# A fourth buffer for incoming weights, paused state chunks, sooner means in the pooling, and seven products in one more MLP group

## The chip, the cores and the metric

The kernel runs on one core of a Trainium2 chip. The metric is the time on the device in microseconds (us), the median of several runs. The engines are called PE (TensorE, the matrix multiplier), PEld (its weight loads), DVE (VectorE), ACT (ScalarE), POOL (GpSimd) and SP (SyncE, which here only issues DMAs).

## The reference, cut to what matters

Two layers run over 520 columns: 512 tokens of a new prompt and one new token for each of 8 samples. D is 1024, FF is 4096, everything is fp32. Layer 0 mixes the tokens by a gated linear recurrence, layer 1 by causal means over 2, 4, 8 and 16 tokens; after either comes an MLP with a squared ReLU.

```python
def _mlp(x, norm_g, w_up, w_down):
    h = _rmsnorm(x, norm_g)
    a = jnp.square(jax.nn.relu(jnp.einsum('bld,df->blf', h, w_up)))
    return jnp.einsum('blf,fd->bld', a, w_down)

for layer in range(DEPTH):
    if layer % N_MIXERS == 0:
        y, s = _hgrn2(x, s_hgrn[j], ...)      # new recurrent state: 8 samples x 8 heads x 128 x 128
    else:
        y, h = _pool(x, hist_pool[j], ...)    # rmsnorm, means over 2, 4, 8, 16 tokens, per-group map
    x = x + y
    x = x + _mlp(x, mlp_norm[layer], mlp_up[layer], mlp_down[layer])
return _rmsnorm(x, final_norm), ...
```

The outputs are the normed x, the new recurrent states (prompt and samples) and the last normed rows of the pooling.

## The kernel before

**Products.** x lies in SBUF as 8 tiles of 128 rows by 520 columns. A weight chunk is a fp32 tile `w` of 128x1024 (512 KB), loaded from `wall`. To keep fp32 accuracy, ACT casts it to a high part `wh` (L221) and DVE subtracts that to get a low part `wl` (L216); the inputs `u` and `a` are split in the same way. One product of a chunk takes three matmuls (`mm3`, L347 to L351) for each of 8 row blocks and each of two halves of 260 columns: 48 matmuls of 128x260, into an accumulator `acc`, of which two exist (the pool `pa`).

**The MLP.** `mlp` (L889) takes FF in 4 groups of 8 tiles. A group has 8 up products into `t` and `a` (L907 to L910), and then 8 down products; each of these ends with `x <- x + acc` (L917), by which DVE empties an accumulator. Groups that the table `FAST` names make their up products by a seven-product scheme (`fast_part`, L919): two chunks, a pair, give seven weight combinations `wp` (`pair_parts`, L229 to L262, with DVE steps ws L245, ws L249, w L254, ws L257 and the split in `put`, ACT L238 and DVE L239), and the inputs give four sums `T` for each row block (`sums`, L849, spread over the group before). A pair of up products is then 7 `quarter` products of 12 matmuls instead of 2 of 48. `FAST` is (2, 3) for the first layer and (1, 2, 3) for the second: five of eight groups. The first up products of the second layer's MLP run column half by half beside the pooling's windows.

**What sets the order.** The PE order is the written order. So is SP's in most of the first layer's MLP (while `steady` is open): SP issues its DMAs one after the other, and one that must wait for a buffer or for data holds up all that stand behind it. DVE and ACT go in the order that a scheduler gives the written code; on the chip each is again a fixed queue. The written order comes from ticks: after every 12 matmuls (every quarter, or a quarter of a product) `tick` (L298) calls `top_up` (L268), which issues loads, splits or the next step of a weight pair, and advances the side tasks of `mix` (L105), each of which may ask to be called again some ticks later. Raw weights have three buffers (`rp`, L143); `top_up` loads a chunk when fewer than two raw chunks wait and fewer than three of the buffers are held (L280). Once a pair's two chunks are there, its steps are written.

**State chunks.** `new_states` (L695) is a side task beside the first layer's MLP. It updates the samples' states in 16 chunks. A chunk is: the load of `st` (L702) and two broadcast fills `bc` (L705) on SP; after STATE[0] ticks three POOL operations (L707 to L709); after STATE[1] more ticks the store `ss_o` (L711) on SP, with which the next chunk's loads are written at once. STATE is (7, 4).

**Pooling.** After the first layer's last down products, column half by half, `after_mlp0` (L1145) starts `pool_half(h)` three ticks after a half is done: the mean's matmul (L413), square root (L417) and reciprocal (L418), and then the windows (`windows`, L1078, from L1084 on), which DVE works through.

Of the kernel before, what the change touches and what calls it, by code (L numbers as in the profile page):

```python
# [7 lines left out]
F32 = mybir.dt.float32  # L8
# [22 lines left out]
SUMS = 2  # L31
SLOTS = 24
EXTRA = 2
FAST = (2, 3), (1, 2, 3)
PAIR = 2
# [3 lines left out]
SAMPLE, LAST_SAMPLE = (4, 4, 4, 1, 1), (5, 2, 3, 0, 1)  # L39
STATE = (7, 4)  # L40
EARLY = 2
# [97 lines left out]
def _kernel(ctx, tc, wall, xT, vec, kst, msk, s0, hist, y_o, sp_o, ss_o, pp_o, ps_o):  # L139
# [49 lines left out]
    depth = [DEPTH]  # L189

    def load():
        if order:
            i, parts = order.pop(0)
            if parts is None:
                w = pp.tile([P, NT, P], F32, name="poolw", bufs=2)
                pool_w.append(w)
            else:
                w = rp.tile([P, NT, P], F32, name="w")
                raw.append((w, parts))
            nc.sync.dma_start(w, wall[i].rearrange("p (k m) -> p k m", m=P))  # L200
# [67 lines left out]
    def top_up():  # L268
        while True:
# [6 lines left out]
            elif raw and raw[0][1] == PAIR and len(raw) > 1:  # L276
                making.append(pair_parts())
            elif raw and raw[0][1] != PAIR and ready() < depth[0] and (room >= 2 or not raw[0][1]):
                split()
            elif order and len(raw) < 2 and len(raw) + halved[0] + len(whole_w) + held_w[0] < 3:  # L280
                load()
            else:
                break
# [408 lines left out]

    drs = []

    def new_states():  # L695

        NH = NB // 2
        for h in range(H):
            for a in range(2):
# [4 lines left out]
                for n, t in ((1, tf), (2, tk)):  # L704
                    nc.sync.dma_start(t, drs[h][n * NB + a * NH:n * NB + (a + 1) * NH, :P].unsqueeze(0).broadcast_to([P, NH, P]))  # L705
                yield STATE[0]
                nc.gpsimd.tensor_tensor(st, st, tf, op=ALU.mult)  # L707
                nc.gpsimd.tensor_tensor(tk, tk, v8[:, h, b].unsqueeze(2).broadcast_to([P, NH, P]), op=ALU.mult)
# [134 lines left out]
    sctx, steady = ExitStack(), ExitStack()  # L843
    sn = sctx.enter_context(tc.tile_pool(name="states", bufs=1))
    states = [True]
    mix.spawn(new_states(), 8)
    steady.enter_context(tc.manual_schedule(engines={mybir.EngineType.SP}))

    def sums(ts, u, step):  # L849
# [6 lines left out]

        def whole_part(k, h, name):
            f = pair_pool[0].tile([P, HT], F32, name=name)
            nc.vector.tensor_tensor(f, *(p[:, span(h)] for p in u[k]), op=ALU.add)  # L859
            return f  # L860

        for j in range(NT // 2):
            b12, f = whole_part(j, 1, "b12"), whole_part(j, 0, "b11")
            nc.vector.tensor_tensor(f, b12, f, op=ALU.subtract)
            put(0, f)
            yield step
            b22 = whole_part(j + NT // 2, 1, "b22")
            nc.vector.tensor_tensor(f, b22, f, op=ALU.subtract)
# [4 lines left out]
            yield step  # L873
            b21 = whole_part(j + NT // 2, 0, "b22")
            nc.vector.tensor_tensor(b21, b21, f, op=ALU.subtract)
# [13 lines left out]
    def mlp(u, r, after, full, fast, apart=None, between=None):  # L889

        ts = [[] for _ in range(4)]
        for g in range(NF // G):
            if g == fast[0] - 1 and not apart:
                open_pairs()
# [66 lines left out]
            if g in fast:  # L961
                assert len(ts[3]) == NT // 2
                for m in range(0, G, 2):
                    fast_part(m)
            elif g == 0 and apart:
                for h in range(2):
# [10 lines left out]
            else:  # L977
                for m in range(G):
                    up_part(m, None)()
            last = g == NF // G - 1  # L980
            if last:
# [3 lines left out]
            if g == 0 and apart:  # L985
                close_pool()
                open_pairs()
                mix.spawn(sums(ts, u, 1), 2)
            for m in range(full if last else NT):
# [155 lines left out]
    def after_mlp0(m, h):  # L1145
# [5 lines left out]
        if len(done[h]) == NT:  # L1151
            mix.spawn(pool_half(h), 3)

# [99 lines left out]
```

## Time and profile before

| | before |
| --- | --- |
| time, median of 3 runs | 1107.88 us (1107.70 to 1108.51) |
| profiled execution: its own time | 1108.78 us |
| profiled execution: span, mean granted clock | 1107.0 us, 0.988 |
| PE matmuls busy | 1063.3 us (96%) |
| PE weight loads busy | 1041.9 us (94%) |
| DVE busy | 790.8 us (71%) |
| ACT busy | 509.9 us (46%) |
| POOL busy | 96.9 us (9%) |
| DMA traffic | 128.11 MB, mean 116 GB/s |

The profile is of one execution; its times are counted from the start of the span. A row of the timeline gives start, duration, engine, line, operation, `out<-in` and shape; in brackets stands how long the engine had been idle before it and which event ended that. "SPq" is the issue of DMAs from SP's queue. In the windows "x" counts instructions and PEclk is the mean granted clock of PE, 1.00 being 2.4 GHz. In the first layer's MLP group 0 has its up products up to about 381 and its down products up to about 427; group 1 goes on to 526, group 2 to 622, group 3 to about 721.

### The profile page before, as it was taken

How to read it: one execution, taken by the hardware profiler on the slowest of the kernel's cores; microseconds unless marked ns; L12 is line 12 of the kernel's file. 1: busy time of each engine (PE TensorE's matmuls, PEld its weight loads, DVE VectorE, ACT ScalarE, POOL GpSimd, SP SyncE). 2: the span in 40 equal slices, each digit the busy share in tenths (PEclk: the TensorE clock that was granted, in tenths of full speed). 3: DMA queues.
4: the chain of work that ended last, by engine and by line, in shares of the span. 5: the costliest groups of instructions: out<-in, count | busy, mean ns of one | idle time of the engine just before them, and what ended most of it. 6: DMA issues, size and time to landing. Idle time of an engine off the chain costs nothing. (4 is left out here: it accounts for less than half of the span.)

```text
span 1107.0 us, 21169 instructions
## 1 busy us (share of the span) xinstructions
PE 1063.3 (96%) x8458; PEld 1041.9 (94%) x8458; DVE 790.8 (71%) x1652; ACT 509.9 (46%) x1174; POOL 96.9 (9%) x145
## 2 busy tenths in 40 slices
PE   9899999899999999999998999997999999999996
PEld 8899999889999999999998999986999999999996
DVE  7898888888679543547864785789958747847845
ACT  6545554444455422332551465546626625625642
POOL 1011101010001221223121000000000000000000
PEclk9999999999999999998999999998999999999998
DMA  8233233223234573464363245034422422422312
GB/s 272 78 99 118 81 98 111 78 87 113 74 104 120 165 228 93 138 203 131 115 210 107 75 131 174 20 99 152 152 77 97 138 73 95 120 85 70 130 38 78
DMA packets 67170, 128.11 MB, mean 116 GB/s; under 512 B 8256, under 2 KB 36608, under 8 KB 67072
## 3 DMA queue, kind: packets, MB, share of 16 engines
q1 hardware_dynamic: 67072, 126.77, 36.0%
q8 instruction: 66, 1.08, 0.4%
q14 instruction: 32, 0.26, 0.1%
HBM read 119.71 MB, written 7.50 MB: 115 GB/s over the span
## 5 line engine op out<-in xcount | busy, mean ns | idle before, releaser
L351 PE MATMUL acc<-u,wh 128*128 128x260 f32 x1344 | 222.9, 288 | 1.1 <-ACT u L389 0.8
L351 PE MATMUL acc<-a,wh 128*128 128x260 f32 x1120 | 183.4, 286 | 7.8 <-DVE x L917 4.2
L351 PEld LDWEIGHTS acc<-u,wh 128*128 128x128 f32 x1344 | 185.2, 188 | 2.5 <-ACT u L389 1.0
L216 DVE TENSOR_TENSOR wl<-w,wh 128x512 fp32r<-128x512 f32 x216 | 149.1, 722 | 30.9 <-ACT wh L221 30.5
L351 PEld LDWEIGHTS acc<-a,wh 128*128 128x128 f32 x1120 | 156.7, 192 | 8.4 <-DVE x L917 4.4
L221 ACT CAST wh<-w 128x512 fp32r<-128x512 f32 x216 | 122.5, 617 | 66.5 <-DMA w<-wall 47.4
L351 PE MATMUL acc<-u,wl 128*128 128x260 f32 x672 | 134.9, 282 | 0.0
L351 PE MATMUL acc<-a,wl 128*128 128x260 f32 x560 | 114.1, 286 | 0.0
L351 PEld LDWEIGHTS acc<-u,wl 128*128 128x128 f32 x672 | 103.2, 188 | 0.0
L351 PEld LDWEIGHTS acc<-a,wl 128*128 128x128 f32 x560 | 87.9, 192 | 0.0
L351 PE MATMUL acc<-T,wp 128*128 128x260 f32 x600 | 81.0, 284 | 2.8 <-ACT R L932 2.8
L917 DVE TENSOR_TENSOR x<-x,acc 128x520 f32<-128x520 f32 x48 | 33.3, 693 | 68.6 <-PE acc L351 68.4
L351 PEld LDWEIGHTS acc<-T,wp 128*128 128x128 f32 x600 | 75.3, 188 | 3.8 <-ACT R L932 3.2
L351 PE MATMUL acc<-a,wx 128*128 128x260 f32 x624 | 76.8, 282 | 0.0
L351 PEld LDWEIGHTS acc<-a,wx 128*128 128x128 f32 x624 | 75.6, 188 | 0.0
L351 PE MATMUL pr<-a,wh 128*128 128x260 f32 x384 | 72.6, 290 | 1.1 <-ACT a L942 0.7
L351 PEld LDWEIGHTS pr<-a,wh 128*128 128x128 f32 x384 | 60.8, 192 | 1.9 <-ACT a L942 0.9
L238 ACT CAST wp<-w 128x512 fp32r<-128x512 f32 x60 | 36.1, 618 | 44.1 <-PE acc L351 43.2
L351 PE MATMUL pr<-a,wl 128*128 128x260 f32 x192 | 54.8, 285 | 0.0
L941 ACT ACTIVATE t<-t 128x260 f32<-128x260 f32 x80 | 32.5, 418 | 46.6 <-DVE t L940 46.4
L568 DVE COPY_PREDICATED A<-mt,pr 128x192 f32<-128x192 uint8 x144 | 47.4, 356 | 7.2 <-PE pr L563 3.9
L238 ACT CAST wp<-ws 128x512 fp32r<-128x512 f32 x50 | 30.4, 619 | 43.9 <-PE acc L351 22.3
(244 smaller groups left out, 2002.7 us busy)
## 6 DMA issues: line engine op xcount, KB each, us to landing
w<-wall SPq DMA_DIRECT2D x179, 512.0 KB, 3.4
st<-s SPq DMA_DIRECT2D x32, 256.0 KB, 3.7
bc<-rows SPq DMA_DIRECT2D x32, 256.0 KB, 6.8
bc<-rows SPq DMA_DIRECT2D x16, 258.0 KB, 3.5
ss_o<-st SPq DMA_DIRECT2D x16, 256.0 KB, 4.2
x<-xT SPq DMA_DIRECT2D x8, 260.0 KB, 5.3
y_o<-y SPq DMA_DIRECT2D x8, 260.0 KB, 2.7
poolw<-wall SPq DMA_DIRECT2D x2, 512.0 KB, 4.4
```

What stands on the lines that cost most here:

```text
L216: nc.vector.tensor_tensor(wl[:, k], w[:, k], wh[:, k], op=ALU.subtract)
L221: nc.scalar.copy(wh[:, k], w[:, k])
L238: nc.scalar.copy(w[:, k[0]], t)
L351: nc.tensor.matmul(o, lhs[a], r[b], start=first and n == 0, stop=last and n == 2, skip_group_check=more)
L568: nc.vector.copy_predicated(Av[:, jj * kk:(jj + 1) * kk, d:4, :].rearrange("p k s b -> p k (s b)"), mv[:, :, s:s + n, :].rearrange("p k s ...
L917: nc.vector.tensor_tensor(xs, xs, acc, op=ALU.add)
L941: nc.scalar.activation(t, t, AF.Square)
```

## The change

- The raw weights get a fourth buffer, `wr` (RAWS), from the pool of the state chunks, in turn with the three of `w`; `top_up` counts four buffers, so one chunk more may wait. At the first layer's last group it is taken back.
- `FAST` of the first layer becomes (1, 2, 3): group 1 also goes by seven products, six of eight groups in all. Its pairs, and the sums of the inputs, are therefore made during group 0.
- While a group's seven products are written, the list `busy` is not empty, and `new_states` asks again every tick before it writes a chunk's POOL operations.
- STATE goes from (7, 4) to (4, 3): a chunk takes 7 ticks instead of 11.
- The pooling's means start 2 ticks (first half) and 1 tick (second half) after a half is done, instead of 3.
- The second layer's sums of the inputs start 7 ticks after the first group's up products instead of 2, and take their scratch from the tile `R` of the pool `mp`.

```diff
+RAWS = 1
-FAST = (2, 3), (1, 2, 3)
+FAST = (1, 2, 3), (1, 2, 3)
-STATE = (7, 4)
+STATE = (4, 3)
...
+    raws = [lambda: rp.tile([P, NT, P], F32, name="w")] * 3
+    loads = [0]
...
-                w = rp.tile([P, NT, P], F32, name="w")
+                w = raws[loads[0] % len(raws)]()
+                loads[0] += 1
...
-            elif order and len(raw) < 2 and len(raw) + halved[0] + len(whole_w) + held_w[0] < 3:
+            elif order and (order[0][1] is not None or pp) and len(raw) < len(raws) - 1 and len(raw) + halved[0] + len(whole_w) + held_w[0] < len(raws):
...
+    busy = []
...
                 yield STATE[0]
+                while busy:
+                    yield 1
                 nc.gpsimd.tensor_tensor(st, st, tf, op=ALU.mult)
...
     sn = sctx.enter_context(tc.tile_pool(name="states", bufs=1))
+    raws += [lambda: sn.tile([P, NT, P], F32, name="wr", bufs=RAWS)] * RAWS
+    loads[0] %= 3
...
-        def whole_part(k, h, name):
-            f = pair_pool[0].tile([P, HT], F32, name=name)
+        def whole_part(k, h):
+            f = mp.tile([P, HT], F32, name="R", bufs=3)
...
         for g in range(NF // G):
+            last = g == NF // G - 1
+            if last and len(raws) > 3:
+                del raws[3:]
+                loads[0] %= 3
...
+                busy.append(True)
                 for m in range(0, G, 2):
                     fast_part(m)
+                busy.clear()
...
-                mix.spawn(sums(ts, u, 1), 2)
+                mix.spawn(sums(ts, u, 1), 7)
...
-            mix.spawn(pool_half(h), 3)
+            mix.spawn(pool_half(h), 2 - h)
```

**SP's queue, first layer, group 0's down products.** Here `w<-wall` and `wr<-wall` are weight loads, `st<-s` and `bc<-rows` the fills of a state chunk, `ss_o<-st` its store. Of the kernel before, from the fourth store on:

```order
L200 DMA w<-wall 128x1024 x2
L711 DMA ss_o<-st 128x512
L702 DMA st<-s 128x512
L705 DMA bc<-rows_1370 128x4x128 x2
L200 DMA w<-wall 128x1024 x3
L711 DMA ss_o<-st 128x512
L702 DMA st<-s 128x512
L705 DMA bc<-rows_1370 128x4x128 x2
L200 DMA w<-wall 128x1024 x3
L711 DMA ss_o<-st 128x512
```

Of the changed kernel, the first store here is the fifth; the loads of one `w` and one `wr` behind it and its fills are the first pair of group 1's, and the two loads in the last row, behind the seventh store, are its second:

```order
L719 DMA ss_o<-st 128x512
L708 DMA st<-s 128x512
L711 DMA bc<-rows_1370 128x4x128 x2
L205 DMA w<-wall 128x1024
L205 DMA wr<-wall 128x1024
L719 DMA ss_o<-st 128x512
L708 DMA st<-s 128x512
L711 DMA bc<-rows_1807 128x4x128 x2
L719 DMA ss_o<-st 128x512
L708 DMA st<-s 128x512
L711 DMA bc<-rows_1807 128x4x128 x2
L205 DMA w<-wall 128x1024 x2
```

Before, two or three weight loads stand between one state store and the next; now there are two or none, and the loads of a pair of group 1 stand behind a store and its fills.

**DVE's queue, the same place.** `x<-x,acc` empties the accumulator of a down product, `wl` is the low part of a weight, `ws`, `w<-w` and `wr<-w` are steps of a weight pair and `wp` its low parts. Of the kernel before, from the first emptying on:

```order
L216 TENSOR_TENSOR wl<-w,wh 128x512 x4
L917 TENSOR_TENSOR x<-x,acc 128x520
L216 TENSOR_TENSOR wx<-w,wx 128x512 x2
L216 TENSOR_TENSOR wl<-w,wh 128x512 x2
L917 TENSOR_TENSOR x<-x,acc 128x520
L216 TENSOR_TENSOR wl<-w,wh 128x512 x2
L917 TENSOR_TENSOR x<-x,acc 128x520
L216 TENSOR_TENSOR wl<-w,wh 128x512 x2
L917 TENSOR_TENSOR x<-x,acc 128x520
```

Of the changed kernel, from the second emptying to the fourth:

```order
L931 TENSOR_TENSOR x<-x,acc 128x520
L244 TENSOR_TENSOR wp<-w,wp 128x512
L250 TENSOR_TENSOR ws<-wr 128x512
L254 TENSOR_TENSOR ws<-ws,w 128x512
L259 TENSOR_TENSOR wr<-w,wr 128x512
L931 TENSOR_TENSOR x<-x,acc 128x520
L244 TENSOR_TENSOR wp<-ws,wp 128x512 x2
L262 TENSOR_TENSOR ws<-w,ws 128x512
L931 TENSOR_TENSOR x<-x,acc 128x520
```

And from the fifth to the sixth:

```order
L931 TENSOR_TENSOR x<-x,acc 128x520
L221 TENSOR_TENSOR wl<-w,wh 128x512 x2
L244 TENSOR_TENSOR wp<-w,wp 128x512
L250 TENSOR_TENSOR ws<-w 128x512
L259 TENSOR_TENSOR w<-w 128x512
L931 TENSOR_TENSOR x<-x,acc 128x520
```

Steps of weight pairs, each of which reads raw chunks that SP loads, now stand between the emptyings: `ws<-wr` (L250) of the first pair ahead of the third emptying, and `ws<-w` (L250) of the second pair ahead of the sixth.

**PE's queue, at the pooling.** `pr<-u,w` are the second layer's first products in fp32 matmuls (L363 of before), `pr<-sqs,mean_w` the means and `acc<-zp,poolw` the pooling's maps. Of the kernel before, from the first layer's last product on:

```order
L351 MATMUL pr<-a,wx 128x260 x24
L363 MATMUL pr<-u_8157,w 128x260 x8
L413 MATMUL pr<-sqs,mean_w 128x260
L1069 MATMUL acc<-zp,poolw 128x268 x4
L363 MATMUL pr<-u_8157,w 128x260 x4
L413 MATMUL pr<-sqs,mean_w 128x260
L363 MATMUL pr<-u_8157,w 128x260 x4
L1069 MATMUL acc<-zp,poolw 128x268 x4
L363 MATMUL pr<-u_8157,w 128x260 x48
```

Of the changed kernel, from the same product on:

```order
L356 MATMUL pr<-a,wx 128x260 x24
L368 MATMUL pr<-u_8241,w 128x260 x4
L418 MATMUL pr<-sqs,mean_w 128x260 x2
L368 MATMUL pr<-u_8241,w 128x260 x4
L1084 MATMUL acc<-zp,poolw 128x268 x4
L368 MATMUL pr<-u_8241,w 128x260 x8
L1084 MATMUL acc<-zp,poolw 128x268 x4
L368 MATMUL pr<-u_8241,w 128x260 x48
```

The two matmuls of the means now stand side by side, where eight matmuls of the next product and four of a map lay between them.

## Rows read from the trace of the kernel before

**Rows 1.** The page: span, busy time by engine, and the weight loads.

```profile
span 1107.0 us, 21169 instructions
PE 1063.3 (96%) x8458; PEld 1041.9 (94%) x8458; DVE 790.8 (71%) x1652; ACT 509.9 (46%) x1174; POOL 96.9 (9%) x145
...
w<-wall SPq DMA_DIRECT2D x179, 512.0 KB, 3.4
```

**Rows 2.** Timeline of PE, where its three longest waits in this MLP end.

```profile
500.13 1.20 PE L351 MATMUL acc<-a,wh 128*128 128x260 f32 x4 [3.61 <-ACT wp L238]
...
555.36 1.71 PE L351 MATMUL acc<-T,wp 128*128 128x260 f32 x12 [2.46 <-ACT R L932]
...
597.52 0.75 PE L351 MATMUL acc<-a,wh 128*128 128x260 f32 x4 [4.24 <-DVE x L917]
```

**Rows 3.** Windows: us, busy by engine, granted clock, DMA share, GB/s.

```profile
500.00:504.00 4.00, 3.87 (x18) 3.90 (x19) 4.00 (x6) 0.09 (x1) 2.28 (x2) 0.50 0.48 127
504.00:508.00 4.00, 4.00 (x26) 4.00 (x26) 1.53 (x2) 0.00 (x0) 2.59 (x2) 0.71 0.27 102
596.00:600.00 4.00, 2.48 (x15) 2.48 (x16) 4.00 (x7) 0.00 (x0) 0.31 (x1) 0.81 0.17 66
600.00:604.00 4.00, 4.00 (x28) 4.00 (x28) 1.08 (x2) 0.00 (x0) 0.00 (x0) 0.76 0.41 131
```

**Rows 4.** Timeline of DVE ahead of the first and third of these waits.

```profile
498.69 0.69 DVE L245 TENSOR_TENSOR ws<-w 128x512 f32<-128x512 f32 x1 [3.97 <-DMA w<-wall]
499.30 0.69 DVE L917 TENSOR_TENSOR x<-x,acc 128x520 f32<-128x520 f32 x1
...
594.30 0.89 DVE L245 TENSOR_TENSOR ws<-w 128x512 f32<-128x512 f32 x1 [9.65 <-DMA w<-wall]
```

**Rows 5.** Timeline of POOL and DVE in group 2's seven products.

```profile
547.59 1.29 POOL L707 TENSOR_TENSOR st<-st,bc 128x512 f32<-128x512 f32 x1 [24.68 <-DMA bc<-rows]
...
547.85 1.32 DVE L943 TENSOR_TENSOR a<-t,a 128x260 fp32r<-128x260 f32 x1
...
553.79 0.42 DVE L943 TENSOR_TENSOR a<-t,a 128x260 fp32r<-128x260 f32 x1
```

**Rows 6.** Timeline of PE in group 0; the chain at a quarter product.

```profile
404.41 0.64 PE L351 MATMUL acc<-a,wh 128*128 128x260 f32 x4
...
427.41 0.64 PE L351 MATMUL acc<-u,wh 128*128 128x260 f32 x4
...
837.22 1.44 PE pr L351 x12
```

**Rows 7.** Timeline of SP: issues of state stores and weight loads.

```profile
351.31 6.00 SPq L200 DMA_DIRECT2D w<-wall  x3
...
387.21 0.38 SPq L711 DMA_DIRECT2D ss_o<-st  x1
...
389.38 3.04 SPq L200 DMA_DIRECT2D w<-wall  x2
399.80 0.34 SPq L711 DMA_DIRECT2D ss_o<-st  x1
...
411.04 0.34 SPq L711 DMA_DIRECT2D ss_o<-st  x1
...
586.25 0.57 SPq L200 DMA_DIRECT2D w<-wall  x1
```

**Rows 8.** Timeline of PE and DVE at the pooling; one window behind it.

```profile
721.31 3.67 PE L363 MATMUL pr<-u,w 128*128 128x260 f32 x16
...
725.97 1.78 DVE L418 RECIPROCAL r<-rs 128x260 f32<-128x260 f32 x1 [0.89 <-ACT rs L417]
...
729.97 1.78 DVE L418 RECIPROCAL r<-rs 128x260 f32<-128x260 f32 x1 [1.69 <-ACT rs L417]
...
731.94 2.54 DVE L1084 TENSOR_TENSOR pe<-pe,r 128x520 f32<-128x520 f32 x3
...
790.00:795.00 5.00, 5.00 (x44) 5.00 (x44) 5.00 (x14) 3.37 (x8) 0.00 (x0) 1.00 0.51 181
```

More of the change, by code (lines that the diff above doesn't have):

```diff
@@ L862, in sums @@
         for j in range(NT // 2):
-            b12, f = whole_part(j, 1, "b12"), whole_part(j, 0, "b11")
+            b12, f = whole_part(j, 1), whole_part(j, 0)
             nc.vector.tensor_tensor(f, b12, f, op=ALU.subtract)
@@ L866, in sums @@
             yield step
-            b22 = whole_part(j + NT // 2, 1, "b22")
+            b22 = whole_part(j + NT // 2, 1)
             nc.vector.tensor_tensor(f, b22, f, op=ALU.subtract)
@@ L873, in sums @@
             yield step
-            b21 = whole_part(j + NT // 2, 0, "b22")
+            b21 = whole_part(j + NT // 2, 0)
             nc.vector.tensor_tensor(b21, b21, f, op=ALU.subtract)
@@ L979, in mlp @@
                     up_part(m, None)()
-            last = g == NF // G - 1
             if last:
```

## The prediction, written before the changed kernel was run

> **What bounds the kernel now.** I read the page first: TensorE (PE) is busy for 1063.3 of 1107.0 us [rows 1], so time is won where PE has fewer matmuls or waits less. Next the waits of PE by length, then its timeline around each. In the first MLP three matter: 3.61 us ending at 500.13 (group 1, down products), 2.46 us ending at 555.36 (group 2, seven products) and 4.24 us ending at 597.52 (group 2, down products) [rows 2]. In the windows of 4 us behind the first the granted clock is 0.50 and 0.71, around the third 0.81 and 0.76 [rows 3]: these stretches run partly at 1.2 GHz. As work at half speed that loses 4 x (0.50 + 0.29) = 3.2 us and at most 4 x (0.19 + 0.24) = 1.7 us.
>
> What made the waits is not what the releaser's name says. At 498.69 VectorE (DVE) starts L245, the first step of a weight pair, after 3.97 us of waiting for the pair's second load; behind it stands L917, which empties the accumulator of the third down product and ends at 499.99 [rows 4]. Two such accumulators exist, so the fifth product can't start before that, and it starts at 500.13 [rows 2]. The third wait is the same: L245 at 594.30 had waited 9.65 us for its load [rows 4]. So the rule that I use below: a down product starts about 0.15 us after the L917 of the product two before it, and that L917 starts only when the pair's load ahead of it in DVE's order has landed. The middle wait has another cause: a DVE operation that takes 0.42 us takes 1.32 there [rows 5], while GpSimd (POOL) works on a state chunk.
>
> **The change, part by part.**
>
> *Seven products in group 1.* A pair of up products costs 2 x 48 matmuls, now 7 x 12. Four products of 48 run from 404.41 to 427.41, 5.75 us each; a quarter product of 12 takes 1.44 in the chain [rows 6]. Gain: 8 x 5.75 - 28 x 1.44 = 5.7 us. DVE and ScalarE get more to do there, as in group 3 of before, for which the list of waits names nothing inside the seven products; so I cost it at nothing. If that cover goes, the price is the 2.5 us that group 2 paid. The sums of the inputs stand at the same place in DVE's order as before (ahead of group 0's first product), so they cost nothing either.
>
> *Pause of the states.* No chunk is asked for during seven products, so the 2.46 us of group 2 go. But the wait stands in the order in which instructions are written, not on the chip: a chunk whose fills were issued just before the group has its POOL operations as soon as the fills land, inside the group. That happens at the start of groups 1 and 2: between nothing and 2.5 us each. I take 1.0 in all, nearer nothing, because DVE has no backlog yet at a group's start. The Trainium skill (SBUF — State Buffer, "Who interferes with whom") says that a GpSimd operation that reads SBUF and a DVE one with two SBUF inputs lock each other out for the whole instruction. That fits the longer operation of rows 5; by it an early chunk would hold DVE for most of its POOL time, and the pause would gain less than I say.
>
> *Fourth buffer.* A load can go out one product earlier. Behind group 2's down products fewer chunks are left, and in group 1 POOL is done with its first chunk when SP gets there. So I let the 3.61 and 4.24 us go with their clock: 3.6 + 3.2 + 4.2 + 1.7 = 12.7 us. If they stay, all of it is lost.
>
> *States at 4 and 3 ticks instead of 7 and 4, in group 0.* A tick is 1.44 us of PE, so a chunk is due every 7 ticks = 10.1 us instead of 15.8. SP takes its queue in order: store of the last chunk, three fills, one or two weight loads, and then the next store, which waits for POOL, which waits for the fills [rows 5]. Where that loop ran freely before, its stores went out at 387.21, 399.80 and 411.04: 12.6 and 11.2 us a turn [rows 7]. So the loop can't keep 10.1, and everything behind it in SP's queue falls back. The ledger:
> - Three weight loads went out behind the first fills between 351.31 and 357.31, when DVE freed their buffers [rows 7]. Two are left ahead of the first store, so it goes at about 355.
> - A turn of 11.5 us (between the two, nearer the shorter, since some turns now carry fewer weights) puts the fifth store at 355 + 4 x 11.5 = 401 and the seventh at 424.
> - Group 1's first pair of loads now stands behind the fifth store and its fills, the second pair behind the seventh. Store and fills take 2.2 us to issue (387.21 to 389.38), the pair's first load 0.4, so the second load of each pair is issued at 403.6 and 426.6. A load behind fresh fills lands 8.0 us later (586.25 to 594.30) [rows 4, 7]; the median of all is 3.4 [rows 1]. I take 8.0: 411.6 and 434.6.
> - In DVE's new order L250 (L245 of before) of the first pair stands ahead of the third L917 of group 0's down products, that of the second pair ahead of the sixth. From landing to the end of L917 it took 1.3 us [rows 4]; one or two more steps of 0.6 stand between now, so 2.0. PE wanted to start the fifth product at 404.41 [rows 6]; it starts at about 414. It wanted to start the eighth at 427.41 - 5.75 = 421.7; it starts at 434.6 + 2.0 = 436.6.
> - So PE is 14.9 us late at the end of group 0, and with a clock loss like the smaller of the two above (1.7) 16.6. The first wait and its clock are contained in that. With turns of 11.2 and 12.6 it is 14.8 and 23.2.
>
> *Pooling.* The means' matmul of the second half now stands next to the other one, half a product of fp32 matmuls (16 in 3.5 us [rows 8], so 1.8) earlier. The two reciprocals start at 725.97 and 729.97, and the windows at 731.94 [rows 8]. Back to back the second would start at 725.97 + 1.7 = 727.7, so 2.3 us earlier, at most 2.3 + 1.8 = 4.1, if the sums are ready. DVE is the engine without a gap from there on, at 790 still [rows 8], so PE's waits there move with it. At worst PE waits at the two matmuls and nothing is gained; I take 2.5, near the lower working. The sums at delay 7 instead of 2 stand among the same DVE work: nothing.
>
> Sum: -5.7 - 2.5 + 1.0 - 12.7 + 16.6 - 2.5 = -5.8. The profiled execution took 1108.78, 1.78 more than its span; the median shown is 0.9 less, 1107.88. So 1107.0 - 5.8 + 1.78 - 0.9 = 1102.1.
>
> **Rivals.**
> - *The state loop keeps up.* Four weight buffers hide it, or loads land in the median 3.4 us. For it: PE had no wait in group 0 before. Against: rows 7. Then the 16.6 falls away: 1107.9 - 22.4 = 1085.5.
> - *The loop costs more than all gains (slower).* Place: SP's queue in group 0. Turns of 12.6 us, the first of rows 7, make PE 23.2 late; and as group 1's down products carry chunks at the same pace, the old wait of 3.6 + 3.2 stays there. -5.8 + 6.6 + 6.8 = +7.6: 1115.5. It decides from 22.4 us of lateness on, turns of 12.5 us with nothing else changed. Against: some turns have no weights.
> - *The pause doesn't pause.* The chunks issued early fall into the seven products at the full 2.5 each, and the pooling gains nothing: -5.8 + 4.0 + 2.5 = +0.7: 1108.6.
>
> **How the numbers follow.** Forecast 0.45 (its own range, with turns of 11.2 to 12.0 and pooling of 0 to 4: 1098 to 1108), loop keeps up 0.25, slower 0.20, no pause 0.10. A measurement of this kernel can tell about 0.2%, 2.2 us, from no change. Faster than that: the first rival and 0.8 of the forecast, 0.61; slower: the slower rival and a bit of the others, 0.22; the same: 0.17. A tenth left out on either side: 1085 to 1113.
>
> **What would show it.** Right: a wait of PE near 404 of 8 to 12 us and another near 430, with DVE L250 waiting for a weight load; state stores 11 to 12 us apart; PE late by some 17 us at the end of group 0, by 11 after group 1's seven products, and no wait over 2 us from there to the end of group 2; windows of the second half 2 to 4 us nearer to the last down product. Wrong: no wait of PE in group 0 (then loads land sooner than 8 us behind the fills, or DVE's order doesn't bind), or long waits in groups 1 and 2.

## The result and the profile after

The changed kernel is slower: 1116.50 us median (1111.46 to 1118.41, 6 runs) against 1107.91 (1103.58 to 1108.51, 6 runs), a ratio of 1.0076 with an interval of 1.0050 to 1.0102. The forecast was 1102.1 us, faster, with a range of 1085 to 1113. The page of its profiled execution (time 1111.46):

```profile
span 1109.7 us, 21166 instructions
PE 1059.5 (95%) x8410; PEld 1037.7 (94%) x8410; DVE 812.5 (73%) x1708; ACT 520.9 (47%) x1214; POOL 95.4 (9%) x145
```

PE is busy for 3.8 us less than before [rows 1] and the span is 2.7 us longer: PE waits more. The timeline of PE, with the waits over 2 us of the first layer's MLP and the one at 434:

```profile
414.42 1.23 PE L356 MATMUL acc<-a,wh 128*128 128x260 f32 x4 [9.40 <-DVE x L931]
434.39 0.74 PE L356 MATMUL acc<-a,wh 128*128 128x260 f32 x4 [0.61 <-DVE x L931]
490.14 0.51 PE L356 MATMUL acc<-a,wh 128*128 128x260 f32 x1 [3.18 <-DVE a L957]
545.53 1.71 PE L356 MATMUL acc<-T,wp 128*128 128x260 f32 x12 [2.44 <-DVE t L953]
585.31 0.39 PE L356 MATMUL acc<-a,wh 128*128 128x260 f32 x1 [2.26 <-DVE a L957]
```

The old waits in the down products [rows 2] are gone; one has come in group 0, one at the start of either group's down products, and the one in group 2's seven products stands at another quarter, behind another operation. The windows behind the first show the clock (columns as in [rows 3]):

```profile
408.00:412.00 4.00, 0.00 (x0) 0.00 (x0) 1.25 (x2) 0.62 (x1) 2.30 (x2) 0.54 0.33 131
412.00:416.00 4.00, 1.58 (x7) 1.59 (x8) 3.93 (x7) 2.28 (x4) 0.00 (x0) 0.50 0.75 224
416.00:420.00 4.00, 4.00 (x26) 4.00 (x25) 3.87 (x4) 0.00 (x0) 3.32 (x3) 0.68 0.15 43
```

In the wait and behind it, 1.2 GHz is granted for most of the first window, all of the second and part of the third: the third has 26 matmuls, where 4 us at full clock hold 35 or 36.

**The wait in group 0, step by step.** SP's timeline shows the loop of the state chunks:

```profile
399.70 0.34 SPq L719 DMA_DIRECT2D ss_o<-st  x1
400.13 0.38 SPq L708 DMA_DIRECT2D st<-s  x1
400.57 1.00 SPq L711 DMA_DIRECT2D bc<-rows  x2
401.61 0.50 SPq L205 DMA_DIRECT2D w<-wall  x1
402.16 0.74 SPq L205 DMA_DIRECT2D wr<-wall  x1
411.30 0.34 SPq L719 DMA_DIRECT2D ss_o<-st  x1
411.74 0.38 SPq L708 DMA_DIRECT2D st<-s  x1
412.17 0.99 SPq L711 DMA_DIRECT2D bc<-rows  x2
421.05 0.35 SPq L719 DMA_DIRECT2D ss_o<-st  x1
```

The fifth store leaves at 399.70, the seventh at 421.05; the first was at 355.65, so a turn took 10.9 us on average. The sixth store, at 411.30, waits for POOL's third operation, and POOL for the fills:

```profile
408.90 1.04 POOL L716 TENSOR_TENSOR bc<-bc,v 128x512 f32<-128x512 f32 x1 [1.69 <-DMA bc<-rows]
410.02 1.26 POOL L717 TENSOR_TENSOR st<-st,bc 128x512 f32<-128x512 f32 x1
```

The first pair's two loads leave at 401.61 and 402.16, right behind store and fills. ACT and DVE at this place:

```profile
410.10 0.62 ACT L243 CAST wp<-w 128x512 fp32r<-128x512 f32 x1 [9.21 <-DMA w<-wall]
```
```profile
410.75 1.07 DVE L244 TENSOR_TENSOR wp<-w,wp 128x512 fp32r<-128x512 f32 x1 [16.51 <-ACT wp L243]
411.75 0.68 DVE L250 TENSOR_TENSOR ws<-wr 128x512 f32<-128x512 f32 x1
...
413.67 0.69 DVE L931 TENSOR_TENSOR x<-x,acc 128x520 f32<-128x520 f32 x1
...
432.31 0.69 DVE L250 TENSOR_TENSOR ws<-w 128x512 f32<-128x512 f32 x1 [7.50 <-DMA w<-wall]
...
433.65 0.69 DVE L931 TENSOR_TENSOR x<-x,acc 128x520 f32<-128x520 f32 x1
```

DVE did nothing for 16.5 us, and from 399.1 on the third product was done and waited to be emptied: its L931 stands behind the pair's first steps. The wait ended at L244, which needs ACT's cast of the pair's first load (410.10); the second load landed at 411.29, while L244 ran, so L250 follows without a wait. L931 ended at 414.36, and PE started at 414.42. At the second pair (432.31) it is L250 that waits for its load.

**The end of a pause.** POOL and DVE at the end of group 1's seven products, two timelines:

```profile
482.67 1.85 POOL L715 TENSOR_TENSOR st<-st,bc 128x512 f32<-128x512 f32 x1 [38.49 <-DMA bc<-rows]
484.49 1.49 POOL L716 TENSOR_TENSOR bc<-bc,v 128x512 f32<-128x512 f32 x1
```
```profile
482.68 2.39 DVE L221 TENSOR_TENSOR wx<-w,wx 128x512 fp32r<-128x512 f32 x2
485.00 1.26 DVE L957 TENSOR_TENSOR a<-t,a 128x260 fp32r<-128x260 f32 x1
486.18 3.57 DVE L221 TENSOR_TENSOR wl<-w,wh 128x512 fp32r<-128x512 f32 x4
489.68 0.76 DVE L957 TENSOR_TENSOR a<-t,a 128x260 fp32r<-128x260 f32 x2
```

The chunk that the pause put off comes back just when DVE must finish the group's last `a`. Undisturbed, two splits take 1.29 (at 493.03), four twice that and an `a` 0.43 (at 469.84); here it is 2.39, 3.57 and 1.26, 2.9 us more, and PE waits 3.18 for the last `a`. The Trainium skill (SBUF — State Buffer, "Who interferes with whom") has one of the two engines wait for the whole of the other's instruction; the trace agrees: the pair of splits ends at 485.07, half a microsecond after POOL's first operation (484.52), and the `a` at 486.26, just after the second (485.98).

**Stage by stage.** Durations in us on PE, from the first matmul of a stage to the first of the next, read from the timelines. "Up" and "down" are the products of a group; "rest" is from the end of the first layer's MLP to the end of the span. The forecast column splits the prediction's terms (its 1.0 for early chunks in halves).

| | to g0 down | g0 down | g1 up | g1 down | g2 up | g2 down | g3 | rest | span |
| --- | --- | --- | --- | --- | --- | --- | --- | --- | --- |
| before | 381.4 | 46.0 | 46.0 | 52.6 | 43.9 | 52.3 | 99.2 | 385.7 | 1107.0 |
| changed | 381.8 | 58.4 | 41.9 | 51.0 | 45.1 | 50.0 | 99.4 | 382.1 | 1109.7 |
| difference | +0.4 | +12.4 | -4.1 | -1.6 | +1.2 | -2.3 | +0.2 | -3.6 | +2.7 |
| forecast | 0 | +16.6 | -5.2 | -6.8 | -2.0 | -5.9 | 0 | -2.5 | -5.8 |
| e1 states as before | 381.9 | 46.0 | 41.2 | 48.2 | 44.9 | 49.7 | 99.6 | 382.0 | 1093.6 |
| e2 on POOL's queue | 389.2 | 46.0 | 45.6 | 46.4 | 40.7 | 46.0 | 99.5 | 381.5 | 1094.9 |
| e3 three buffers | 382.1 | 58.2 | 41.6 | 51.0 | 40.5 | 48.3 | 99.2 | 382.4 | 1103.2 |
| e4 no pause | 383.4 | 61.0 | 47.4 | 55.0 | 40.7 | 46.0 | 99.2 | 382.2 | 1114.9 |
| e5 changed again | 382.0 | 60.2 | 42.2 | 50.8 | 46.7 | 50.3 | 99.3 | 381.3 | 1112.8 |
| e6 STATE 5, 4 | 382.7 | 53.4 | 40.7 | 50.2 | 40.7 | 47.4 | 102.9 | 381.8 | 1099.8 |
| e7 e1, three buffers | 380.9 | 46.0 | 48.9 | 48.1 | 44.9 | 50.4 | 99.3 | 381.5 | 1100.0 |
| e8 POOL's queue, late | 381.0 | 46.0 | 51.5 | 47.5 | 40.7 | 46.0 | 99.6 | 382.3 | 1094.6 |
| e9 five groups | 381.9 | 47.7 | 46.0 | 63.1 | 40.7 | 46.0 | 99.1 | 381.4 | 1106.0 |
| e10 e1, five groups | 381.7 | 46.0 | 46.0 | 46.3 | 43.1 | 46.0 | 99.1 | 381.1 | 1089.2 |
| e11 pooling alone | 381.9 | 46.0 | 46.0 | 50.9 | 41.9 | 52.3 | 99.2 | 378.1 | 1096.3 |
| e12 POOL's queue, held | 381.5 | 46.0 | 40.7 | 48.8 | 41.4 | 50.3 | 102.1 | 382.6 | 1093.3 |
| e13 e10, old sums | 382.8 | 46.0 | 46.0 | 46.1 | 43.1 | 46.0 | 99.2 | 378.3 | 1087.5 |
| e14 e13, delay 7 | 382.0 | 46.0 | 46.0 | 46.0 | 43.3 | 46.0 | 99.2 | 378.6 | 1087.0 |
| e15 e1, old sums | 381.8 | 46.0 | 41.6 | 47.0 | 44.2 | 50.4 | 99.5 | 379.2 | 1089.7 |
| e16 e13, POOL's queue | 382.7 | 46.0 | 46.0 | 47.5 | 40.7 | 46.0 | 99.2 | 378.2 | 1086.2 |

The smallest values are 46.0 for eight full products and some 40.5 for seven-product groups; what is above them is wait and clock. Each row is one execution. Where two kernels have the same code up to a place, their rows differ by up to 2 us in a stage (before and e11 up to group 3, the changed kernel and e5), so a difference of 1 or 2 us in one stage shows little by itself.

### The profile page after: what moved, and what is told of

The parts are those of the page before. It is cut to its first block, busy times and chain, and to the rows that moved or that the text cites. A ratio compares the mean times of both kernels' runs of the same rounds, so it can differ in the third digit from the quotient of the medians.

```text
span 1109.7 us, 21166 instructions
## 1 busy us (share of the span) xinstructions
PE 1059.5 (95%) x8410; PEld 1037.7 (94%) x8410; DVE 812.5 (73%) x1708; ACT 520.9 (47%) x1214; POOL 95.4 (9%) x145
## 4 chain that ended last, share of the span: by engine, by line
PE 44%; DVE 6%; DMA 2%; issue 1%; ACT 1%; SPq 0%; DVEq 0%; ACTq 0%
PE acc L356 26%; PE pr L356 16%; PE acc L1084 1%; DVE wl L221 1%; DMA w<-wall 1%; DMA wr<-wall 1%; DVE s L1106 1%; DVE wp L244 0%; DVE a L957 0%; DVE r L423 0%; DVE t L921 0%; DVE a L924 0%; DVE sqs L410 0%; DVE u L395 0%; DVE t L954 0%
## 5 line engine op out<-in xcount | busy, mean ns | idle before, releaser
L356 PE MATMUL acc<-u,wh 128*128 128x260 f32 x1184 | 198.1, 289 | 0.8 <-ACT u L394 0.4
L356 PEld LDWEIGHTS acc<-u,wh 128*128 128x128 f32 x1184 | 164.2, 189 | 2.1 <-ACT u L394 0.6
L221 DVE TENSOR_TENSOR wl<-w,wh 128x512 fp32r<-128x512 f32 x198 | 135.0, 714 | 12.7 <-ACT wh L226 12.4
L226 ACT CAST wh<-w 128x512 fp32r<-128x512 f32 x198 | 112.2, 617 | 65.5 <-PE acc L356 32.7
L356 PE MATMUL acc<-u,wl 128*128 128x260 f32 x592 | 119.2, 283 | 0.0
L356 PE MATMUL acc<-T,wp 128*128 128x260 f32 x708 | 95.9, 285 | 4.2 <-DVE t L953 2.6
L356 PEld LDWEIGHTS acc<-T,wp 128*128 128x128 f32 x708 | 88.7, 188 | 6.2 <-DVE t L953 3.1
L356 PEld LDWEIGHTS acc<-u,wl 128*128 128x128 f32 x592 | 91.2, 189 | 0.0
L931 DVE TENSOR_TENSOR x<-x,acc 128x520 f32<-128x520 f32 x48 | 33.3, 694 | 70.1 <-PE acc L356 70.1
L356 PE MATMUL pr<-u,wp 128*128 128x260 f32 x432 | 57.6, 282 | 0.0
L244 DVE TENSOR_TENSOR wp<-w,wp 128x512 fp32r<-128x512 f32 x65 | 45.0, 703 | 16.6 <-ACT wp L243 16.5
```

The costliest lines, as they stand in the source:

```text
L221: nc.vector.tensor_tensor(wl[:, k], w[:, k], wh[:, k], op=ALU.subtract)
L226: nc.scalar.copy(wh[:, k], w[:, k])
L244: nc.vector.tensor_tensor(w[:, k[1]], t, w[:, k[0]], op=ALU.subtract)
L356: nc.tensor.matmul(o, lhs[a], r[b], start=first and n == 0, stop=last and n == 2, skip_group_check=more)
L931: nc.vector.tensor_tensor(xs, xs, acc, op=ALU.add)
```

## The experiments

e1 to e4, e5 to e8, e9 to e12 and e13 to e16 each shared a chip and 7 to 14 runs of the kernel before, whose medians were 1107.61, 1106.48, 1107.01 and 1105.95; across these groups kernels are compared by their ratios to it. All edits are to the changed kernel unless another is named.

**e1. State chunks as before.**

```diff
-STATE = (4, 3)
+STATE = (7, 4)
-                while busy:
-                    yield 1
```

> The changed kernel, with the state chunks as they were (STATE 7 and 4, no pause). Theory A (the loop of store, fills and POOL, 11 us a turn, holds up the pair loads behind it on SP): PE's wait of 9.4 us at 414 shrinks below 2 us, group 1 starts before 431 instead of at 440.25, and the waits at the first down products of groups 1 and 2 (3.2 and 2.3 us), where the paused chunks came back, go too; 1097 to 1104 us. Rival B (the steps of the weight pairs in DVE's queue are the cost, whoever sends the loads): DVE's queue in group 0 is the same here, so the wait near 414 stays at 7 us or more and the time at 1111 us or more.

Measured: 1094.64 us, ratio 0.9878 (0.9856 to 0.9900), 2 us under the range expected. The wait near 414 is gone, though DVE's order in group 0 is the same: group 1 starts at 427.96. Theory A holds: the two edits to the chunks cost more than all others gain. The first pair's loads stand right behind store and fills here too, and its second one lands at 400.27, 9.3 us after its issue; but the store is the third, not the fifth, and so they leave 11 us sooner:

```profile
387.72 0.42 SPq L717 DMA_DIRECT2D ss_o<-st  x1
...
390.99 1.31 SPq L205 DMA_DIRECT2D wr<-wall  x1
```

So what costs is how many turns of the loop SP must finish ahead of the pair. What is left, on PE:

```profile
505.82 0.74 PE L356 MATMUL acc<-a,wh 128*128 128x260 f32 x4 [1.39 <-DVE x L929]
...
539.07 2.74 PE L356 MATMUL acc<-T,wp 128*128 128x260 f32 x12 [2.74 <-DVE t L951]
...
569.10 0.39 PE L356 MATMUL acc<-a,wh 128*128 128x260 f32 x1 [1.96 <-DVE a L955]
```

So a wait of 2 us behind group 2's seven products is there without a pause as well, where theory A had it go: a chunk happens to fall on DVE's last splits there (POOL from 562.09 to 566.01). That of group 1 has shrunk to 0.33.

**e2. The chunks' DMAs on POOL's queue.**

```diff
-                nc.sync.dma_start(st, s0[:, h, b])
+                nc.gpsimd.dma_start(st, s0[:, h, b])
...
-                nc.sync.dma_start(ss_o[:, h, b], st)
+                nc.gpsimd.dma_start(ss_o[:, h, b], st)
```

> The changed kernel, with the chunks' loads, fills and stores issued by POOL instead of SP; STATE and the pause as changed, DVE's and PE's queues the same. Theory A: no weight load stands behind a store any more, the waits at 414 and 434 go, group 1 starts before 431; 1100 to 1107 us. Rival B: wait near 414 stays, no change against 1116. Rival C (what costs is the traffic of the chunks at the faster pace, not the queue): loads behind fills still land 8 us after their issue, and group 1 starts at 435 or later; 1109 to 1116 us.

Measured: 1099.78 us, ratio 0.9935 (0.9911 to 0.9959). Group 0's down products take 46.0 us with the same order on DVE and PE and with chunks running beside them, so it was SP's queue, and neither the traffic nor DVE's order alone. (Weight loads behind others still take 6 to 7 us there, as from 397.62 to 403.95, but they leave in time.) The group started 7.4 us later than in the changed kernel: on POOL's queue nothing holds the chunks back, and they run from before 330 on, beside the input sums that DVE makes there. PE has a wait of 7.0 us at the mean's matmul, which the trace puts down to no engine; it went when the chunks were held back (e8).

**e3. Three buffers.**

```diff
-RAWS = 1
+RAWS = 0
```

> The changed kernel with three weight buffers (RAWS 0). Theory A: the fourth buffer is not the cause; with one less the pair loads go out later, the wait in group 0 stays at 9 us or more, and the waits at loads in the down products of groups 1 and 2 come on top: 1116 to 1126 us. Rival D (the fourth buffer lets loads and splits pile up ahead of what PE needs): waits in group 0 below 4 us, 1111 us or less.

Measured: 1105.12 us, ratio 0.9978 (0.9967 to 0.9988): 11 us faster than the changed kernel. The expectation of theory A failed; rival D has the time, but not the place. Group 0 takes as long as with four buffers, in two waits, the first behind a plain split (DVE L221 at 401.47), the second behind a pair's first low part (L244 at 414.22):

```profile
403.95 8.40 PE L356 MATMUL acc<-a,wx 128*128 128x260 f32 x48 [4.48 <-DVE x L931]
...
415.57 0.79 PE L356 MATMUL acc<-a,wh 128*128 128x260 f32 x4 [3.23 <-DVE x L931]
```

What the profiles show of the gain, 6.5 us between the spans, is in group 2: 40.5 and 48.3 instead of 45.1 and 50.0. The other 4 us are in executions without a trace. In group 2 the changed kernel had a step of a pair on DVE ahead of what PE waits for:

```profile
540.63 0.69 DVE L250 TENSOR_TENSOR ws<-wr 128x512 f32<-128x512 f32 x1 [4.52 <-DMA wr<-wall]
...
541.84 0.69 DVE L931 TENSOR_TENSOR x<-x,acc 128x520 f32<-128x520 f32 x1
```

It reads the fourth buffer, whose load left at 532.52 behind fresh fills. With three buffers this step comes behind that emptying, and PE has no wait over 0.6 us in these seven products.

**e4. No pause.** Only the two lines of the `while` are taken out.

> The changed kernel without the pause, STATE 4 and 3. Theory A: group 0 as in the changed kernel (group 1 starts at 438 to 442). The waits at the first down products of groups 1 and 2, 3.2 and 2.3 us with a fall of the clock, go, because no chunk waits for the end of the pause; chunks inside group 1's seven products cost 1 to 2.5 us each, up to four of them. Together 1110 to 1117 us. Rival E (the pause pays as meant): slower than the changed kernel by 3 us or more, 1119 or more.

Measured: 1115.49 us, ratio 1.0074 (1.0056 to 1.0093), as the changed kernel within its spread. Group 0 takes 61.0 us, so its loss is the pace's and not the pause's. Groups 1 and 2 together take 189.1 us instead of 188.0: what the pause saves in group 1 (47.4 and 55.0) it loses in group 2, which is clean without it. Rival E falls: the pause doesn't pay.

**e5. The changed kernel once more.**

> The changed kernel as it is, to see what the usual execution has that the first profile (span 1109.7, with a time 5 us under the median of 1116.5) had not. Theory A: the waits stand at the same places (414 in group 0, the first down products of groups 1 and 2, the start of group 2's seven products), and are longer or bring a lower clock: group 1 starts at 440 to 447; 1114 to 1118 us. Rival: the additional time lies outside the first layer's MLP, and group 3 starts at 628 as in the first profile.

Measured: 1117.45 us, ratio 1.0092 (1.0074 to 1.0110). The waits stand at the same places; group 1 starts at 442.21, 2 us later than in the first profile:

```profile
416.32 1.23 PE L356 MATMUL acc<-a,wh 128*128 128x260 f32 x4 [11.18 <-DVE x L931]
```

In both profiles the execution was the quickest of its kernel's runs (1111.46 and 1114.56), so the last 3 to 5 us up to the medians are in no trace. Where they go stays open.

**e6. STATE 5 and 4, pause in groups 1 and 2 only.**

```diff
-STATE = (4, 3)
+STATE = (5, 4)
...
+                if not last:
                     busy.append(True)
```

> The changed kernel with STATE 5 and 4 (9 ticks, 13.0 us a chunk, where the loop on the chip takes 11.0) and the pause in groups 1 and 2 only. Theory A (the pace of 10.1 us that the loop can't keep is what costs): the wait near 414 falls below 3 us, group 1 starts before 432, the waits at the first down products behind a pause stay (2 to 3 us each); 1100 to 1106 us. Rival F (not the pace, but that chunks and pair loads share SP's queue at all): wait near 414 of 6 us or more, 1110 us or more.

Measured: 1099.30 us, ratio 0.9932 (0.9909 to 0.9954). In time within 1 us of what theory A said; in the profile half a miss:

```profile
410.62 1.23 PE L356 MATMUL acc<-a,wh 128*128 128x260 f32 x4 [4.74 <-DVE x L931]
```

The wait is halved, not under 3 us, and group 1 starts at 436.06, not before 432. The waits expected behind the pauses did not come: none over 0.11 us stands there. The pair's loads left at 397.70 and 398.25, right behind fresh fills, and DVE's first step of the pair (L244) ran at 406.95. The loop took 12.1 us a turn up to there (stores from 358.98 to 407.51), less than the 13.0 asked of it. So a loop that is in time still puts a load behind fills, as rival F has it; the pace decides how late.

**e7. States as before, three buffers.** The edits of e1 and e3.

> The changed kernel with the state chunks as they were (as in the first experiment, 1094.6) and three weight buffers. Theory A2 (the fourth buffer only does harm when SP is late, because it puts steps that need a load earlier into DVE's queue; with SP in time it does what it was meant to): slower than 1094.6 by 3 to 10 us, 1098 to 1105. Rival D2 (the fourth buffer costs in any case, as the 11 us between the changed kernel and its version with three buffers say): 1085 to 1093 us.

Measured: 1103.17 us, ratio 0.9966 (0.9952 to 0.9980), against 0.9878 with four, as theory A2 expected: the fourth buffer gains some 10 us here. With the quick chunks it costs 11. So the sign of one edit hangs on another. In the profiles the gain is 6.4 us, and it stands in group 1's seven products (41.2 for 48.9), not in the down products for which it was forecast (together 97.9 for 98.5).

**e8. As e2, with a late start.** Of the first chunk's three tiles POOL writes one column from `r` ahead of the fills.

```diff
+                if h == 0 and a == 0:
+                    for t in (st, tf, tk):
+                        nc.gpsimd.tensor_tensor(t[:, 0, 0:1], r[:, 0:1], r[:, T - 1:T], op=ALU.add)
                 nc.gpsimd.dma_start(st, s0[:, h, b])
```

> The chunks' DMAs on POOL's queue as in the second experiment, but the first chunk waits for r, the reciprocals at about 350 us (POOL writes one column of its three tiles from r before the fills; the fills overwrite it). In the second experiment chunks began before that and PE waited 7.0 us at 344. Theory A: that wait falls below 1 us, group 1 starts before 431, chunks run through group 1's seven products at 1 to 5 us in all, groups 2 and 3 are free of waits over 1 us; 1085 to 1092 us. Rival C (traffic): no gain over 1099.8, the wait moves to a weight load in group 0.

Measured: 1095.93 us, ratio 0.9905 (0.9890 to 0.9920), over the range expected. The 7 us are gone and groups 2 and 3 are clean, as expected, but chunks in group 1's seven products cost 11 us, not 1 to 5:

```profile
462.26 2.97 PE L356 MATMUL acc<-T,wp 128*128 128x260 f32 x12 [3.13 <-ACT R L949]
```

This is one of three such waits there (1.7, 1.8, 3.1), and the clock falls behind them.

**e9. Five groups, quick chunks.**

```diff
-FAST = (1, 2, 3), (1, 2, 3)
+FAST = (2, 3), (1, 2, 3)
```

> The changed kernel with the first layer's FAST back at (2, 3), the chunks at the new pace. Theory A2 (the late loads cost because steps of weight pairs, which need two chunks, stand ahead of the emptyings in DVE's queue): no pair is made in group 0, the wait near 414 falls below 3 us, group 1 starts before 432 and takes 46 us for its up products instead of 42; 1106 to 1113 us. Rival G (any load that SP sends late holds PE, pairs or not): PE waits 6 us or more in group 0 all the same, 1117 us or more.

Measured: 1108.39 us, ratio 1.0018 (1.0006 to 1.0030). Time and wait in group 0 are as theory A2 said (1.4 us), but the loss came back in group 1's down products, on PE and on DVE:

```profile
493.44 6.79 PE L356 MATMUL acc<-a,wx 128*128 128x260 f32 x39 [6.10 <-DVE x L931]
...
504.89 1.21 PE L356 MATMUL acc<-a,wh 128*128 128x260 f32 x4 [3.59 <-DVE x L931]
```
```profile
491.03 1.74 DVE L221 TENSOR_TENSOR wl<-w,wh 128x512 fp32r<-128x512 f32 x2 [9.04 <-ACT wh L226]
492.70 0.68 DVE L931 TENSOR_TENSOR x<-x,acc 128x520 f32<-128x520 f32 x1
```

Here a plain split, not a pair's step, stands ahead of the emptying, and its load is late: it left at 482.23, right behind fills, and ACT's cast of it began at 490.38. So rival G has a part: any step that needs a late load will do.

**e10. e1 with five groups.** The edits of e1 and e9.

> The kernel of the first experiment (state chunks as before, 1094.6) with FAST of the first layer back at (2, 3). This prices the seven products in group 1 by themselves. By the prediction's term of 5.7 us, of which the first experiment's profile shows 4.8 (41.2 us of up products instead of 46.0): 1098 to 1101 us. Rival: the pairs cost in DVE and SP what they save on PE, 1093 to 1096 us.

Measured: 1091.53 us, ratio 0.9868 (0.9848 to 0.9887), against 0.9878 of e1, faster than both expectations. The term of 5.7 us falls: the seven products save 4.8 us where they run (41.2 for 46.0), and groups 1 and 2 lose 7.4 behind them (48.2, 44.9 and 49.7 instead of 46.3, 43.1 and 46.0). By the ratios six groups gain nothing. And here the term for the old waits holds: the down products of groups 1 and 2 take 12.6 us less than before (46.3 and 46.0 for 52.6 and 52.3), where 12.7 were forecast; e11, with three buffers, has 50.9 and 52.3.

**e11. The pooling alone**, in the kernel before.

```diff
-            mix.spawn(pool_half(h), 3)
+            mix.spawn(pool_half(h), 2 - h)
```

> The kernel before with only the means of the pooling sooner (2 and 1 ticks instead of 3). The prediction's term is 2.5 us, the changed kernel's profile shows 3.5 from group 3's end to the end: 1103 to 1105.5 us. Rival: in the kernel before the windows wait for something else, no change, 1106 to 1108.5 us.

Measured: 1099.37 us, ratio 0.9932 (0.9908 to 0.9956): 7.5 us, three times the term, and faster than both expectations. Its "rest" is 7.6 us shorter than before's, that of the changed kernel only 3.6. In either the means stand back to back and the first window operation comes 6.5 us after the MLP's end instead of 10.6 (in the changed kernel 734.17 for 727.64, before 731.94 for 721.31). Before, PE then waited for 6.1 us in eight pieces, from the second layer's last fp32 products into its first down products, and the clock fell:

```profile
761.00:765.00 4.00, 1.94 (x6) 1.30 (x6) 4.00 (x11) 3.38 (x9) 0.00 (x0) 0.67 0.23 56
765.00:769.00 4.00, 3.66 (x17) 3.49 (x17) 4.00 (x10) 2.75 (x6) 0.00 (x0) 0.50 0.43 139
```

The 4 us between the changed kernel and this one are lost at these first down products. In the changed kernel, on DVE, PE and in the window:

```profile
756.32 0.76 DVE L869 TENSOR_TENSOR R<-u 128x260 f32<-128x260 f32 x2
```
```profile
768.07 1.02 PE L356 MATMUL pr<-a,wx 128*128 128x260 f32 x3 [1.76 <-DVE a L924]
```
```profile
768.00:772.00 4.00, 3.94 (x16) 3.64 (x17) 4.00 (x11) 3.97 (x9) 0.00 (x0) 0.50 0.46 138
```

And in this kernel:

```profile
752.21 1.11 DVE L859 TENSOR_TENSOR b<-u 128x260 f32<-128x260 f32 x3
```
```profile
754.00:758.00 4.00, 2.34 (x15) 1.73 (x14) 4.00 (x10) 3.67 (x10) 0.00 (x0) 1.00 0.61 220
758.00:762.00 4.00, 4.00 (x36) 4.00 (x35) 4.00 (x10) 1.74 (x4) 0.00 (x0) 1.00 0.47 152
```

The sums (`R<-u`, here `b<-u`) start 28.7 us after the MLP's end in the changed kernel and 34.0 here, although the changed kernel writes them later.

**e12. POOL's queue, chunks held on the chip.** As e8, with STATE (5, 3), the first chunk written 14 ticks after its task is spawned instead of 8, the pause in groups 1 and 2 only and ahead of a chunk's fills, and a chunk that met it beginning with the same three operations, reading `x[:, 0, 0:1]` after the group's first down product.

> The chunks' DMAs on POOL's queue, the first chunk held until r is there, and the chunks kept out of the seven products of groups 1 and 2 on the chip: the first chunk behind the pause begins with POOL operations of one column that read x after the group's first down product (its fills overwrite them). STATE 5 and 3, 7 chunks ahead of group 1. The eighth experiment lost 11 us in group 1's seven products (51.5 us instead of 40.5), where chunks ran, and nothing elsewhere. Theory A: these go for the most part, 1083 to 1089 us. Rival: the chunks collide with DVE's work of the down products instead, 1092 us or more.

Measured: 1094.90 us, ratio 0.9895 (0.9877 to 0.9912). The seven products are clean now (40.7 and 41.4), but the down products take 48.8 and 50.3, and group 3, where the last chunks fall, 3 us more: the rival was right. In this arrangement of six groups every place that was tried for the 16 chunks costs something.

**e13 and e14. e10 with the second layer's sums in their old tiles**, at delay 2 and 7.

```diff
-            f = mp.tile([P, HT], F32, name="R", bufs=3)
+            f = pair_pool[0].tile([P, HT], F32, name=name) if parted else mp.tile([P, HT], F32, name="R", bufs=3)
...
-                mix.spawn(sums(ts, u, 1), 7)
+                mix.spawn(sums(ts, u, 1), 2)
```

> The tenth kernel (five groups, chunks as before, 1091.5) with the second layer's sums as before: own scratch tiles in the pool of the pairs, and delay 2. Theory R (the tile R lets the sums start beside the pooling's windows, where DVE has no slack): the wait of 1.8 us and the clock of 0.50 at the second layer's first down products go; 1086 to 1088.5 us. Rival: no change, 1090.5 to 1092.5.

> As the thirteenth, but with delay 7. Theory R: the same as there, within 1 us, since the old tiles come free only after the pooling, whatever the delay. Rival (the delay brings the sums to the wrong place): 1090.5 to 1092.5 us.

Measured: 1090.23 us, ratio 0.9857 (0.9841 to 0.9873), and 1089.39, 0.9849 (0.9834 to 0.9865). Both have a rest of 378.3 and 378.6 us, and no fall of the clock there: theory R holds in the profile, the delay doesn't matter. In time it is 1 to 2 us against e10 by the ratios, less than expected and within the intervals, so by time alone nothing is shown.

**e15. e1 with the old sums**, at delay 2.

> The first kernel (six groups, chunks as before, 1094.6) with the second layer's sums as before, own tiles and delay 2. Theory R: 4 to 5 us faster than 1094.6, 1089.5 to 1091 us, 3 us over the thirteenth. Rival: the six groups' lateness and the sums share their cost, under 2 us gained.

Measured: 1092.33 us, ratio 0.9878 (0.9854 to 0.9902), the ratio of e1 and 1 us over the range expected. Its rest is 2.8 us shorter than e1's, but the median doesn't show it: inconclusive. On the same chip it is 2.1 us over e13, so six groups are again no gain.

**e16. e13 with the chunks on POOL's queue**, started late as in e8, STATE (4, 3).

> The thirteenth kernel with the chunks' DMAs on POOL's queue and the first chunk held until r is there, as in the eighth (STATE 4 and 3). Theory A: the chunks end at about 525 us, in group 1, whose full products leave DVE slack; the waits of 0.9 and 1.1 us in group 2's seven products, where a chunk ran, go with their clock; 1083 to 1086 us. Rival: DVE is locked out more by POOL at the quicker pace, in groups 0 and 1, and waits come there: 1088 us or more.

Measured: 1087.83 us, ratio 0.9836 (0.9815 to 0.9858), 2 us over the range expected, and by its median the fastest kernel here: 18 us under the kernel before on its chip. The interval overlaps those of e13 and e14. The chunks run beside full products, and group 2's seven products are clean (40.7).

## Why the prediction was wrong

- **Group 0: the place and the queue right, the size partly luck.** Stores at 355, 401 and 424 were forecast and came at 355.65, 399.70 and 421.05. The fifth product was forecast for 414 and came at 414.42, but two errors cancel there: the pair's second load left 1.4 us sooner than forecast and took 9.1 us instead of 8.0. DVE's wait stood one step earlier than forecast, ahead of L244 and the pair's first load. The lateness was sized at 16.6 us and was 12.4 to 14.2 (e5): the second pair's load added 0.6 us where 5.3 were forecast (14.9 less 9.6), since a turn took 10.9 us instead of 11.5. e1, e2 and e4 show the cause: the quick chunks on SP's queue.
- **The step that failed: "I let the 3.61 and 4.24 us go with their clock", a term of 12.7 us.** The two waits went, but the down products of groups 1 and 2 gave back 3.9 us in the profile, and the prediction's own sign of being wrong came, long waits in groups 1 and 2. The chunk behind each pause now falls on DVE's last splits, and PE waits 3.18 and 2.26 us there; and behind a late load of the fourth buffer a wait of 2.44 us came in group 2's seven products. The sum asked whether the old waits lose their cause, and not where the quicker chunks and the new pairs come to stand in these groups; only the slower rival did. Without these two edits the size of the term was right: with five groups and the chunks as before the same stages give back 12.6 us (e10), with six groups 7.0 (e1), with the quick, paused chunks 3.9. That the fourth buffer by itself gains some 10 us with six groups (e7 against e1) is near the forecast by luck: in the profiles it gains elsewhere. Behind a late queue it costs 11 (e3). At group 2 the rows show how: a step is written earlier and so stands ahead of an emptying in DVE's fixed order, while its load comes no sooner.
- **The pause: mis-sized.** It was costed at a gain of 1.5 us net. It does keep chunks out of the seven products: with three buffers those of group 2 are clean (40.5, e3), and what they lose in the changed kernel (45.1) stands mostly behind the fourth buffer's load. The prediction saw that a chunk written before the pause runs inside the group, but not that the chunk behind it lands at its end, on DVE's last `a`. e4 shows the sum: nothing.
- **Seven products: right where they run, wrong in sum.** -4.1 for -5.2 in the stage; the cover costed at nothing on DVE was not there (e10).
- **Pooling: mis-sized.** Alone it measures 7.5 us, not 2.5: the windows came 4.1 us nearer, the prediction's upper working, and most of the old waits behind them went, with their clock (e11). "The sums at delay 7 instead of 2 stand among the same DVE work: nothing" failed: the scratch tile R is free at once, where the old tiles, by the code, stand in memory that the pooling holds, so DVE takes the sums up 5 us earlier, among the windows. That takes 2.5 to 2.8 us back in the profile (e13 and e14 against e10).
- **Of the rivals** the slower one (1115.5, a chance of 0.20) came near the median by luck in its main term: it wanted turns of 12.6 us and PE 23.2 us late, and they were 10.9 and 12.4 to 14.2. Its other half held in size: group 1's down products stayed nearly as long (51.0 for 52.6), though behind another operation.
- **What stays open:** the last 3 to 5 us up to the medians are in no trace, and the terms above account for the profiled executions alone.

The terms of the sum were worked out each by itself; those failed in which one edit moves what the gain of another rests on.

## What to carry to other kernels

More lookahead helps only if the queue that feeds it is in time: otherwise it can move work that needs late data ahead of work that is urgent, on an engine that goes in a fixed order. Look, for each in-order queue, at what its slowest loop takes a turn, and keep a steady loop that has its own latency (store, fill, compute) off the queue that feeds the bottleneck. When a tile moves to memory that is free sooner, its work starts sooner, and that may be the wrong time; a wait costs its length and the clock behind it.

## What was not expected of the hardware

- A weight load that leaves right behind fills landed 8.9 us (issued at 482.73 in e9) to 9.3 us (390.99 in e1) later, where the median of all before was 3.4 [rows 1].
- On POOL's queue a DMA takes 0.55 to 0.76 us of POOL to issue, and a chunk's turn there took 9.2 to 11.3 us (stores of e8 from 394.56 to 435.30), no longer than over SP, although POOL now issues four DMAs for each three operations.
- At the second layer's first down products a granted clock of 0.50 for 4 us followed on waits of 2.8 us in three pieces (window at 768 above); e11, with 1.6 us in two, kept 1.00.
